# Plain fp32 products for the small matmuls of a hybrid decoder layer, regrouped between the projections

## The chip, the cores and the metric

The kernel runs on one NeuronCore of one Trainium2 chip. The metric is the device time of one execution, in microseconds (us). The times shown of the kernel before are 987.24, 990.89 and 992.40 us, with a median of 990.89 us. In the text, PE is the matrix engine (TensorE), DVE the vector engine, ACT the scalar engine, POOL the GpSimd engine, and SP the engine whose queue issues most of the transfers.

## The reference, cut to what matters

One decoder layer over 512 tokens plus 16 learned tokens (T = 528), of width 1024. One projection `h @ w_in` feeds two branches. The first is sliding-window attention with 16 query heads over 2 key heads. The second is RWKV-7 time mixing with 16 heads of 64 channels. Sigmoid gates merge the branches, and an output projection, a layer norm and a squared-ReLU MLP follow.

```python
w = -softplus(-(w0 + tanh(wl) @ w2)) - 0.5        # low-rank product, rank 64
a = sigmoid(a0 + al @ a2)                         # low-rank product, rank 64
g = sigmoid(gl) @ g2                              # gate product, rank 128
def step(S, inp):                                 # one token, one head, S is 64 x 64
    sa = einsum('bhij,bhj->bhi', S, -kk_t)
    S = S * w_t + sa * (kk_t * a_t) + v_t * k_t
    return S, einsum('bhij,bhj->bhi', S, r_t)
logits = einsum('nqkgd,nskd->kgnqs', qb, kw) * HEAD_DIM ** -0.5   # attention scores
merged = sigmoid(gate_att) * att + sigmoid(gate_rwkv) * rw
h = layer_norm(ALPHA * h + merged @ w_out)
h = layer_norm(ALPHA * h + square(relu(h @ w_ff1)) @ w_ff2)
```

All inputs are float32.

## The kernel before, in words

**Large products.** Every large matmul is a sum of three products of the type fp32r. Each operand is split into a part `hi` (a cast by ACT) and a rest `lo` (a subtraction by DVE), and `three` adds hi*hi, hi*lo and lo*hi in PSUM. The input projection runs as a generator `dense` for each block of 128 output columns: 24 matmuls of 512 columns for queries and gates, or two spans of 24 matmuls of 264 columns where the 16 extra tokens are needed too (keys, reads, values). Their PSUM tile is `dps`, from a pool `dn` of two banks.

**The recurrence.** It is computed in 8 chunks of 64 tokens, for a pair of heads at a time, so there are 8 pairs j. For a pair, `rwkv_scores` makes the products of scaled keys and queries inside each chunk (tile `sc`), `rwkv_inverse` inverts 16 x 16 triangles by a long row of small DVE instructions (tiles `ftmp`, `Xf`), `rwkv_blocks` joins them to 64 x 64 blocks (`up`), `rwkv_turn_inverse` makes `wp`, and `rwkv_fold` makes `gq` and adds it to `AX`. Then `rwkv_chain` passes a 64 x 64 state through the chunks: a link is two matmuls `ch`, and `follow` scales their results into `Z`, one half on DVE and one on ACT, for the next link.

**Small products beside it.** The low-rank products (`rwkv_lora`) keep hi and lo of an operand on the two halves of the partitions, so that two fp32r matmuls give what three would. The attention scores (`sp`) are made in the same way from `qs` and `khi`, `klo`; for `qs`, four transfers for each pair move halves of `qhi` and `qlo`. The gate product (`gp`) is a `three`. The small matmuls of the recurrence (`sc`, `gq`, `ch`, `wp`, `up`, `meta`, `Y`) are plain fp32, and the trace holds two records, two passes, for each of them. Transposes (`tr`, `axt`, `pt`, `yt`) have one.

**The order.** On PE it is written out by hand. A stage s works on pair s (`scan`), on pair s-1 (`solve`, and the attention scores) and on pair s-2 (attention output). `weave` walks through the stage's projection matmuls and puts each small job in when a running time has reached the job's number. That running time adds a fixed estimate for every projection matmul, so the number is a place among the projections, not a time of the clock. The other engines take their instructions in an order that the framework's scheduler derives, helped by `ahead(...)`.

```python
(5.6, (), F(rwkv_bonus, j)), (12.4, (), F(rwkv_turn_scores, j)),                          # L1395, L1396
(8.4, (), F(rwkv_fold, j, 0)), (10.6, (), F(rwkv_fold, j, 1)),                            # L1413
+ [(11.6 + 0.95 * c, (), F(rwkv_chain, j, c)) for c in range(NCH - 1)]                    # L1415
(7.4, (), F(rwkv_lora, j, 0)), (8.6, (), F(rwkv_lora, j, 1)),                             # L1423
items += attend(s - 1, 9.2) + join(s - 1, 11.6, 25.4, 0)[:2]                              # L1471
```

PSUM has eight banks: two for `dps` (`dn`), two called `g` (pool `pg`: `sc`, `gq`, `bp`, `wp`, `axt`, `tr`, `vt`), two called `a` (pool `pat`: `sp`, `pt`, `av`, `gp`, the low-rank products and some others) and two for the chain.

Of the kernel before, what the change touches and what calls it, by code (L numbers as in the profile page):

```python
# [31 lines left out]
PAIRS = HEADS // 2  # L32
DFF = 4096
# [51 lines left out]
ABUF = {'qs': 1, 'ga': 1, 'gg': 1, 'pa': 1, 'z': 1, 'bv': 1}  # L85
# [45 lines left out]
def hybrid_layer_kernel(ctx: ExitStack, tc: tile.TileContext, I: dict, out: bass.AP):  # L131
# [298 lines left out]
    zw = lz.tile([P, T], F32R, name="zw", tag="zw")  # L430
    za = lz.tile([P, T], F32R, name="za", tag="za")
    sghi = lz.tile([P, SEQ], F32R, name="sghi", tag="sghi")
    sglo = lz.tile([P, SEQ], F32R, name="sglo", tag="sglo")
# [11 lines left out]
    def low_rank(zl):  # L445
        twl = ew.tile([HD, T], F32, name="twl", tag="u")
        act.activation(twl, zl[0:HD], AF.Tanh)
        tal = ew.tile([HD, T], F32, name="tal", tag="L")
        act.copy(tal, zl[HD:P])
        for dst, src in ((zw, twl), (za, tal)):  # L450
            act.copy(dst[0:HD], src)
            dve.tensor_tensor(dst[HD:P], src, dst[0:HD].bitcast(F32), op=ALU.subtract)

    def gate_rank(zg):
        sg = ew.tile([P, SEQ], F32, name="sg", tag="v")
        act.activation(sg, zg[:, NMETA:], AF.Tanh, scale=0.5)
        dve.tensor_scalar(sg, sg, 0.5, 0.5, op0=ALU.mult, op1=ALU.add)
        act.copy(sghi, sg)
        dve.tensor_tensor(sglo, sg, sghi.bitcast(F32), op=ALU.subtract)
# [16 lines left out]
    def rwkv_begin(j):  # L476

        S = SS[j]
        lw = ew.tile([P, 2, P], F32, name="lw", tag="lw")
        lhi = ew.tile([P, 2 * P], F32R, name="lhi", tag="lhi")  # L480
        llo = ew.tile([P, 2 * P], F32R, name="llo", tag="llo")
        lf = lw.rearrange("p a c -> p (a c)")
        nc.sync.dma_start(lf, I["lora"][j])
        act.copy(lhi, lf)
        dve.tensor_tensor(llo, lf, lhi.bitcast(F32), op=ALU.subtract)
        S["lora"] = lhi, llo
# [3 lines left out]
    def rwkv_lora(j, q):  # L490
        S = SS[j]
        lhi, llo = S["lora"]
        zz, dst, bias = ((zw, S["tw"], "w0h"), (za, S["ta"], "a0h"))[q]
        qc = slice(q * P, (q + 1) * P)
        for t0, n in ALLT:
            ps = pat.tile([P, 512], F32, name="dps", tag="a")
            ts_ = slice(t0, t0 + n)
            pe.matmul(ps[:, :n], lhi[:, qc], zz[:, ts_], start=True, stop=False)
            pe.matmul(ps[:, :n], llo[:, qc], zz[:, ts_], start=False, stop=True)
            act.activation(dst[:, ts_], ps[:, :n], AF.Tanh, bias=dcol(bias, j), scale=0.5)  # L500
        if q == 0:
            tw = dst
# [100 lines left out]
    def rwkv_bonus(j):  # L603
# [3 lines left out]
        bp = pg.tile([P, 512], F32, name="bp", tag="g")  # L607
# [46 lines left out]
    def rwkv_scores(j, i):  # L654
# [9 lines left out]
        scs = [pg.tile([P, 512], F32, name="sc", tag="g") for e in range(2)]  # L664
# [7 lines left out]
        q4 = [ps.rearrange("p (c t) -> p c t", c=4) for ps in scs]  # L672
        with ahead(PRI["scores"]):
            for e in range(2):
                R = ER[e]
                dve.tensor_tensor(
                    NT[R, cs, :], q4[e][R, :, 0:C], B64(dv[R, cs], C), op=ALU.mult
                )
            for e in range(2):
                R, K_ = ER[e], ER[1 - e]  # L680
                dve.tensor_tensor(
# [1067 lines left out]
```

## Time and profile before

| what | value |
|---|---|
| median of three runs | 990.89 us |
| the profiled execution's own time | 988.82 us |
| its span | 986.7 us |
| PE busy | 943.9 us, 96% of the span |
| DVE busy | 654.9 us, 66% |
| ACT busy | 455.0 us, 46% |
| granted PE clock | 0.99 |
| low-rank products of a pair, PE records | 8 matmuls of 264 columns |
| attention scores of a pair, PE records | 16 matmuls of 256 columns |
| gate product of a pair, PE records | 3 matmuls of 512 columns |

The span is the time from the first to the last recorded instruction; 2.1 us of the execution's own time lie around it. A row of the groups shows a source line, engine, operation, the tiles (out<-in) and the shape, then the busy time of the group, the mean nanoseconds of one instruction and the idle time of the engine just before the group with what ended it. A row of the timeline shows start, duration, engine, line, operation, tiles, shape and how many instructions are merged in it. Matmuls overlap in the pipeline, so a matmul's duration is longer than its distance to the next one.

### The profile page before, as it was taken

The page shows a single profiled execution, that of the slowest core. Times are in us where ns is not written, and L with a number is a line of the kernel's source. Part 1 is how long each engine was busy: PE and PEld are TensorE (multiplying, and loading weights), DVE is VectorE, ACT ScalarE, POOL GpSimd, SP SyncE. Part 2 cuts the span into 40 slices and gives each one's busy share as a digit, 9 for nine tenths or more (in the row PEclk, how much of TensorE's full clock was granted, in tenths as well). Part 3 has the DMA queues.
Part 4 walks back from the last instruction along what each step waited for, and adds up shares of the span by engine and source line. Part 5 has one row for each costly group of instructions (what it writes and reads, how often), then busy time and mean ns, then how long its engine had stood idle before and what let it go on. Part 6 is the DMA issues. An engine that isn't in the chain of part 4 may idle for free.

```text
span 986.7 us, 19121 instructions
## 1 busy us (share of the span) xinstructions
PE 943.9 (96%) x7557; PEld 790.8 (80%) x7557; DVE 654.9 (66%) x1505; ACT 455.0 (46%) x1130; POOL 45.9 (5%) x108
## 2 busy tenths in 40 slices
PE   4999999999999999999999999999999999999996
PEld 3889878788888887888876778888888888888885
DVE  8677887888887888778786967666523244452427
ACT  6635447465473664654726834644412133442220
POOL 2000000010010000100001001000000000000001
PEclk9999999999999999999999999999999999999998
DMA  7545323233324432242534536133232323223222
GB/s 272 95 131 150 90 73 105 82 77 98 91 74 120 105 98 59 69 111 80 147 116 105 194 114 228 44 122 113 89 103 86 106 86 104 89 88 104 76 96 85
DMA packets 82673, 105.46 MB, mean 107 GB/s; under 512 B 47766, under 2 KB 54664, under 8 KB 82584
## 3 DMA queue, kind: packets, MB, share of 16 engines
q1 hardware_dynamic: 81088, 102.16, 35.0%
q10 hardware_dynamic: 1496, 2.08, 0.6%
q8 instruction: 59, 0.97, 0.4%
q14 instruction: 30, 0.25, 0.1%
HBM read 86.29 MB, written 13.74 MB: 101 GB/s over the span
## 4 chain that ended last, share of the span: by engine, by line
PE 72%; DVE 16%; ACT 5%; DMA 3%; issue 2%; POOL 2%; SPq 0%; DVEq 0%; ACTq 0%; POOLq 0%
PE dps L340 12%; PE dps L341 11%; PE dps L342 11%; PE acc L1518 6%; PE acc L1520 6%; PE acc L1519 6%; DVE wlo L259 3%; DMA wraw<-in_w_in_dram 2%; PE sc L668 2%; PE o L1292 1%; PE av L1196 1%; PE wp L873 1%; POOL grs L973 1%; PE ch L950 1%; PE o L1293 1%
## 5 line engine op out<-in xcount | busy, mean ns | idle before, releaser
L259 DVE TENSOR_TENSOR wlo<-wraw,whi 128x512 fp32r<-128x512 f32 x240 | 158.4, 686 | 178.2 <-ACT whi L256 177.4
L256 ACT CAST whi<-wraw 128x512 fp32r<-128x512 f32 x240 | 140.5, 616 | 271.8 <-PE dps L341 131.2
L340 PE MATMUL dps<-hhi,whi 128*128 128x264 f32 (+1 forms) x640 | 217.7, 340 | 7.3 <-DVE qlo L1074 5.5
L341 PE MATMUL dps<-hlo,whi 128*128 128x264 f32 (+1 forms) x640 | 204.5, 320 | 1.1 <-DVE hlo L321 1.1
L342 PE MATMUL dps<-hhi,wlo 128*128 128x264 f32 (+1 forms) x640 | 204.1, 319 | 0.4 <-DVE wlo L259 0.4
L340 PEld LDWEIGHTS dps<-hhi,whi 128*128 128x128 f32 x640 | 121.5, 190 | 22.2 <-DVE qlo L1074 6.8
L342 PEld LDWEIGHTS dps<-hhi,wlo 128*128 128x128 f32 x640 | 121.4, 190 | 9.1 <-DVE wlo L259 0.6
L341 PEld LDWEIGHTS dps<-hlo,whi 128*128 128x128 f32 x640 | 121.8, 190 | 7.3 <-DVE hlo L321 1.9
L341 PE MATMUL dps<-h1lo,whi 128*128 128x512 f32 (+1 forms) x256 | 97.5, 381 | 0.0
L340 PE MATMUL dps<-h1hi,whi 128*128 128x512 f32 (+1 forms) x256 | 97.5, 381 | 0.0
L342 PE MATMUL dps<-h1hi,wlo 128*128 128x512 f32 (+1 forms) x256 | 97.5, 381 | 0.0
L341 PEld LDWEIGHTS dps<-h1lo,whi 128*128 128x128 f32 x256 | 48.1, 188 | 10.2
L342 PEld LDWEIGHTS dps<-h1hi,wlo 128*128 128x128 f32 x256 | 48.1, 188 | 10.2
L340 PEld LDWEIGHTS dps<-h1hi,whi 128*128 128x128 f32 x256 | 48.1, 188 | 10.2
L1518 PE MATMUL acc<-whi,hhi 128*128 128x512 f32 x128 | 50.6, 395 | 0.0
L1519 PE MATMUL acc<-wlo,hhi 128*128 128x512 f32 x128 | 50.4, 394 | 0.0
L1520 PE MATMUL acc<-whi,hlo 128*128 128x512 f32 x128 | 50.2, 392 | 0.0
L1520 PE MATMUL acc<-whi,flo 128*128 128x512 f32 x112 | 44.0, 393 | 0.0
L1518 PE MATMUL acc<-whi,fhi 128*128 128x512 f32 x112 | 43.8, 391 | 0.0
L1519 PE MATMUL acc<-wlo,fhi 128*128 128x512 f32 x112 | 43.8, 391 | 0.0
L908 ACT ACTIVATE Z<-ch,PC 64x64 f32<-64x64 f32 x56 | 17.4, 310 | 41.0 <-PE ch L950 40.5
L1618 DVE TENSOR_TENSOR rl<-rl 128x512 f32<-128x512 f32 (+1 forms) x36 | 22.8, 632 | 15.2 <-ACT hhi L1617 9.1
(302 smaller groups left out, 1732.6 us busy)
## 6 DMA issues: line engine op xcount, KB each, us to landing
wraw<-in_w_ff_dram SPq DMA_DIRECT2D x64, 512.0 KB, 3.5
wraw<-in_w_in_dram SPq DMA_DIRECT2D x52, 512.0 KB, 3.6
wraw<-in_w_out_dram SPq DMA_DIRECT2D x8, 512.0 KB
xt<-in_x_dram SPq DMA_DIRECT2D x4, 512.0 KB, 7.5
Nd<-NT SPq DMA_DIRECT2D x16, 128.0 KB, 3.0
bv<-bv SPq DMA_DIRECT2D x8, 256.0 KB, 2.1
bvm<-bv SPq DMA_DIRECT2D x8, 256.0 KB
qs<-qhi SPq DMA_DIRECT2D x16, 128.0 KB, 2.2
```

The costliest lines, as they stand in the source:

```text
L256: act.copy(hi[:n, qs], raw[:n, qs])
L259: dve.tensor_tensor(lo[:n, qs], raw[:n, qs], hi[:n, qs].bitcast(F32), op=ALU.subtract)
L340: pe.matmul(ps, whi, xhi, start=first, stop=False)
L341: pe.matmul(ps, whi, xlo, start=False, stop=False)
L342: pe.matmul(ps, wlo, xhi, start=False, stop=last)
L668: pe.matmul(scs[e][:, c * P : (c + 1) * P], BK[ER[e], 4 * i + c, :], AXg[ER[e], e, 4 * i + c], start=True, stop=True,)
L873: pe.matmul(w4[:, c, :], XB[:, 4 * i + c, :], S["AT"][:, 4 * i + c, :], start=True, stop=True,)
L908: act.activation(dst, src[e][ER[e]], AF.Copy, scale=scale)
L1518: pe.matmul(acc[b], xhi[k][:, bs], hi[:, ws], start=first, stop=False)
L1519: pe.matmul(acc[b], xhi[k][:, bs], lo[:, ws], start=False, stop=False)
L1520: pe.matmul(acc[b], xlo[k][:, bs], hi[:, ws], start=False, stop=last)
L1618: dve.tensor_tensor(r, r, r, op=ALU.mult)
```

## The change

It has six parts.

1. **Plain operands.** The low-rank products, the attention scores and the gate product use fp32 operands as they are. `zw`, `za`, `sghi`, `sglo`, `lhi`, `llo`, `gwh`, `gwl`, `khi`, `klo`, `qhi`, `qlo` and `qs` go, with the casts, subtractions and transfers that made them. The two low-rank products stand on the two halves of the partitions, and so do the two heads of a score.
2. **Quarters.** `rwkv_scores` makes its products in 64 x 64 quarters, so that the two head-diagonal quarters share one bank and the other two share the second. Four instructions on 64 partitions (`NT`, `GR`) become two on 128.
3. **Both folds in one place.** For the first seven pairs, the second half of `rwkv_fold` follows the first at once; its two banks come from the pool `pat`.
4. **Places.** The chain starts at 10.6 with a step of 1.05. Low-rank products, gate product, the transposes `axt` and the attention scores have numbers that put them behind a chain link. A score call does two blocks of 128 queries at once, so there are two calls for a pair, not four.
5. **The bonus product** `bp` moves to the place of `wp` and takes its bank from `pat`.
6. **Smaller things.** The value transposes `vp` move to 21.0, and `first_up` uses the new tiles' room.

```diff
-ABUF = {'qs': 1, 'ga': 1, 'gg': 1, 'pa': 1, 'z': 1, 'bv': 1}
+ABUF = {'q': 2, 'ga': 1, 'gg': 1, 'pa': 1, 'z': 1, 'bv': 1}
...
     def low_rank(zl):
-        twl = ew.tile([HD, T], F32, name="twl", tag="u")
-        act.activation(twl, zl[0:HD], AF.Tanh)
-        tal = ew.tile([HD, T], F32, name="tal", tag="L")
-        act.copy(tal, zl[HD:P])
-        for dst, src in ((zw, twl), (za, tal)):
-            act.copy(dst[0:HD], src)
-            dve.tensor_tensor(dst[HD:P], src, dst[0:HD].bitcast(F32), op=ALU.subtract)
+        act.activation(zz[0:HD], zl[0:HD], AF.Tanh)
+        act.copy(zz[HD:P], zl[HD:P])
...
     def rwkv_lora(j, q):
-        for t0, n in ALLT:
-            ps = pat.tile([P, 512], F32, name="dps", tag="a")
-            ts_ = slice(t0, t0 + n)
-            pe.matmul(ps[:, :n], lhi[:, qc], zz[:, ts_], start=True, stop=False)
-            pe.matmul(ps[:, :n], llo[:, qc], zz[:, ts_], start=False, stop=True)
+        t0, n = ALLT[q]
+        pss = [pat.tile([P, 512], F32, name="lps", tag="a") for e in range(2)]
+        for e in range(2):
+            pe.matmul(
+                pss[e][:, :n], S["lora"][ER[e]], zz[ER[e], ts_], start=True, stop=True
+            )
+        for ps, (dst, bias) in zip(pss, outs):
             act.activation(dst[:, ts_], ps[:, :n], AF.Tanh, bias=dcol(bias, j), scale=0.5)
-        if q == 0:
+        if q == 1:
...
-        bp = pg.tile([P, 512], F32, name="bp", tag="g")
+        bp = pat.tile([P, 512], F32, name="bp", tag="a")
...
         for c in range(4):
+            for d in range(2):
+                for e in range(2):
+                    to = ER[e ^ d]
+                    pe.matmul(
+                        scs[d][to, c * P : (c + 1) * P], BK[ER[e], 4 * i + c, to],
+                        AXg[ER[e], e, 4 * i + c], start=True, stop=True,
+                    )
-            for e in range(2):
-                pe.matmul(
-                    scs[e][:, c * P : (c + 1) * P], BK[ER[e], 4 * i + c, :],
-                    AXg[ER[e], e, 4 * i + c], start=True, stop=True,
-                )
...
-            gqs = [pg.tile([P, 512], F32, name="gq", tag="g") for e in range(2)]
+            pool_, tag = ((pg, "g"), (pat, "a"))[i and j < PAIRS - 1]
+            gqs = [pool_.tile([P, 512], F32, name="gq", tag=tag) for e in range(2)]
...
         def evict(ps, t0, n):
             with ahead(PRI["dense"]):
-                act.activation(hi, ps, AF.Copy, scale=HD**-0.5)
-                dve.scalar_tensor_tensor(
-                    lo, ps, HD**-0.5, hi.bitcast(F32), op0=ALU.mult, op1=ALU.subtract
-                )
+                act.activation(q, ps, AF.Copy, scale=HD**-0.5)
...
     def gate_out(j):
-        three(gp, *A["gw", j], sghi, sglo)
+        pe.matmul(gp, A["gw", j], sg, start=True, stop=True)
...
-            pe.matmul(s3[:, e], qs[e][:, blk], khi[:, win], start=True, stop=False)
-            pe.matmul(s3[:, e], qs[e][:, blk], klo[:, win], start=False, stop=True)
+        for d in range(2):
+            n = 2 * i + d
+            for e in range(2):
+                pe.matmul(
+                    sps[e][:, d * 256 : (d + 1) * 256], q[ER[e], n * P : (n + 1) * P],
+                    kk[ER[e], n * P : n * P + 256], start=True, stop=True,
+                )
...
-            (5.6, (), F(rwkv_bonus, j)),
-            (12.4, (), F(rwkv_turn_scores, j)),
+            (6.4, (), F(rwkv_bonus, j)),
+            (12.55, (), F(rwkv_turn_scores, j)),
...
-            (10.6, (), F(rwkv_fold, j, 1)),
-        ] + [(11.6 + 0.95 * c, (), F(rwkv_chain, j, c)) for c in range(NCH - 1)] + [
+            (8.4 + 2.2 * last, (), F(rwkv_fold, j, 1)),
+        ] + [(10.6 + 1.0 * last + 1.05 * c, (), F(rwkv_chain, j, c)) for c in range(NCH - 1)] + [
...
-            (7.4, (), F(rwkv_lora, j, 0)),
-            (8.6, (), F(rwkv_lora, j, 1)),
+            (11.65, (), F(rwkv_lora, j, 0)),
+            (12.7, (), F(rwkv_lora, j, 1)),
...
-                items += [(8.6, (), turn_heads)]
+                items += [(21.0, (), F(turn_heads, s // 4))]
             if 0 < s < PAIRS - 1:
-                items += attend(s - 1, 9.2) + join(s - 1, 11.6, 25.4, 0)[:2]
+                items += attend(s - 1, 14.8) + join(s - 1, 13.75, 25.4, 0)[:2]
```

Three places show how the order moves. The first is PE in a middle stage before the change, from the first half of the fold on; L498 and L499 are the low-rank product of `a`, L340 to L342 are projection matmuls.

```order
L890 MATMUL gq<-GR,WT 128x128 x8
L498 MATMUL dps<-za,lhi 128x264
L499 MATMUL dps<-za,llo 128x264
L498 MATMUL dps<-za,lhi 128x264
L499 MATMUL dps<-za,llo 128x264
L340 MATMUL dps<-hhi,whi 128x512
L341 MATMUL dps<-hlo,whi 128x512
L342 MATMUL dps<-hhi,wlo 128x512
L1138 MATMUL sp<-khi,qs_3938 128x256
```

After the change, the same stage has `gq` with 16 products in one row and no low-rank product near it. The low-rank product `lps` comes behind a later chain link, with the transposes `axt` ahead of the link:

```order
L695 MATMUL axt<-con,AX 128x128 x8
L939 MATMUL ch<-Z,AX 64x64
L939 MATMUL ch_4318<-Z,AX 64x64
L484 MATMUL lps<-zz,lw 128x264 x2
L341 MATMUL dps<-hhi,whi 128x264
L342 MATMUL dps<-hlo,whi 128x264
L343 MATMUL dps<-hhi,wlo 128x264
```

So four small fp32r matmuls among the projections have become two plain products behind a link.

The second place is PE around the gate product `gp`, which follows a chain link in both kernels. Before:

```order
L950 MATMUL ch<-Z,AX 64x64
L950 MATMUL ch_4460<-Z,AX 64x64
L340 MATMUL gp<-sghi,gwh 128x512
L341 MATMUL gp<-sglo,gwh 128x512
L342 MATMUL gp<-sghi,gwl 128x512
```

After the change it is one plain product behind the fourth link:

```order
L939 MATMUL ch<-Z,AX 64x64
L939 MATMUL ch_4318<-Z,AX 64x64
L1088 MATMUL gp<-sg,gw 128x512
L341 MATMUL dps<-hhi,whi 128x264
L342 MATMUL dps<-hlo,whi 128x264
L343 MATMUL dps<-hhi,wlo 128x264
```

The score matmuls `sp`, which stood among the projections behind the first fold, now follow the fifth and the seventh link in the same way.

The third place is DVE in that stage, at the last half of the fold (`AX<-AX,gq`) and the state scaling `Z` of the first chain link. Before:

```order
L775 TENSOR_TENSOR ftmp<-Xf,Nf 66x55
L259 TENSOR_TENSOR wlo<-wraw,whi 128x512
L779 TENSOR_TENSOR Xf<-Xf,ftmp 66x11x5
L1141 TENSOR_TENSOR sb<-sp,bias 128x256
L775 TENSOR_TENSOR ftmp<-Xf,Nf 66x48
L895 TENSOR_TENSOR AX<-AX,gq 128x8x64 x2
L906 TENSOR_SCALAR Z<-ch,PC 64x64
```

Now four additions stand close together, and five steps of the small inverse lie between the last of them and the first `Z`:

```order
L884 TENSOR_TENSOR AX<-AX,gq 128x8x64 x2
L762 TENSOR_TENSOR ftmp<-Xf,Nf 66x64
L766 TENSOR_TENSOR Xf<-Xf,ftmp 66x8x8
L884 TENSOR_TENSOR AX<-AX,gq 128x8x64 x2
L762 TENSOR_TENSOR ftmp<-Xf,Nf 66x63
L766 TENSOR_TENSOR Xf<-Xf,ftmp 66x9x7
L762 TENSOR_TENSOR ftmp<-Xf,Nf 66x60
L766 TENSOR_TENSOR Xf<-Xf,ftmp 66x10x6
L762 TENSOR_TENSOR ftmp<-Xf,Nf 66x55
L895 TENSOR_SCALAR Z<-ch,PC 64x64
```

On PE, six projection matmuls of 264 columns stand between the first and the second chain link after the change, where before the change there were nine and `gp`, `sp` and `axt`.

More of the change, by code (lines that the diff above doesn't have):

```diff
@@ L32 @@
 PAIRS = HEADS // 2
+ATT_GROUP = PAIRS // 2
 DFF = 4096
@@ L478, in rwkv_begin @@
         S = SS[j]
[L479 to L486, printed above, removed]
+        S["lora"] = lw = ew.tile([P, P], F32, name="lw", tag="lw")
+        nc.sync.dma_start(lw, I["lora"][j])
         S["tw"] = ew.tile([P, T], F32, name="tw", tag="tw")
@@ L1117, in evict @@
             A["gg", j] = t
-        A["gw", j] = gwh, gwl
+        A["gw", j] = gw
         yield from dense(COL_GRW + j * P, XT_, evict)
@@ L1402, in solve @@
     def solve(j):
+        last = j == PAIRS - 1
         return [
```

137 lines of the change are left out of this document (51 added, 86 removed).

## The prediction

> **What bounds the kernel now.** I read the page first, then the stages, then PE's groups with their idle time, and last the timeline of one middle stage. The page's first part, its chain, and one of the stretches of 120 us:
>
> ```profile
> PE 943.9 (96%) x7557; PEld 790.8 (80%) x7557; DVE 654.9 (66%) x1505; ACT 455.0 (46%) x1130; POOL 45.9 (5%) x108
> PE 72%; DVE 16%; ACT 5%; DMA 3%; issue 2%; POOL 2%; SPq 0%; DVEq 0%; ACTq 0%; POOLq 0%
> 240.00:360.00 120.00, 116.82 (x1233) 99.71 (x1217) 98.42 (x266) 70.64 (x202) 8.94 (x22) 1.00 0.33 89
> ```
>
> PE works 116.8 of 120 us there at a granted clock of 1.00, and DVE 98.4. So the time of this part is the distance from one PE start to the next, plus the few waits of PE. The change touches nothing behind the output projection. PE's groups show where it waited (the last columns):
>
> ```profile
> L340 PE MATMUL dps<-hhi,whi 128*128 128x264 f32 x448 | 135.8, 303 | 7.3 <-DVE qlo L1074 5.5 <-ACT whi L256 1.1 <-DVE ftmp L775 0.6
> L1138 PE MATMUL sp<-khi,qs 128*128 128x256 f32 x64 | 17.3, 296 | 5.1 <-ACT ta L500 2.7 <-DVE sb L1141 1.8 <-DMA qs<-qlo 0.7
> L1054 PE MATMUL vp<-con,vT 64*128 64x64 f32 x10 | 1.0, 227 | 2.9 <-issue 1.5 <-ACT ta L500 1.5
> L498 PE MATMUL dps<-zw,lhi 128*128 128x264 f32 x16 | 4.4, 292 | 1.4 <-DVE zw L452 1.4
> ```
>
> Two of these return stage by stage; the first twice, a stage apart, with what ended it, and a case of the second:
>
> ```profile
> 230.47 0.60 ACT L1073 ACTIVATE qhi<-dps 128x512 fp32r<-128x512 f32 x1
> 231.12 0.68 DVE L1074 SCALAR_TENSOR_TENSOR qlo<-dps,qhi 128x512 fp32r<-128x512 f32 x1
> 231.86 0.39 PE L340 MATMUL dps<-hhi,whi 128*128 128x264 f32 x1 [0.91 <-DVE qlo L1074]
> 295.60 0.39 PE L340 MATMUL dps<-hhi,whi 128*128 128x264 f32 x1 [0.91 <-DVE qlo L1074]
> 323.19 0.84 ACT L500 ACTIVATE ta<-dps,drv 128x264 f32<-128x264 f32 x2
> 323.71 0.39 PE L1138 MATMUL sp<-khi,qs 128*128 128x256 f32 x1 [0.67 <-ACT ta L500]
> ```
>
> The projection after a query waits until DVE has emptied the query's bank, and the scores wait for a bank of `pat` that the low-rank product still holds.
>
> **Prices.** Plain products, fp32r products and the gaps around an island of small ones:
>
> ```profile
> 314.82 1.95 PE L873 MATMUL wp<-AT,XB 128*128 128x128 f32 x16
> L873 PE MATMUL wp<-AT,XB 128*128 128x128 f32 x128 | 15.6, 275 | 0.0
> 318.52 0.29 PE L498 MATMUL dps<-zw,lhi 128*128 128x264 f32 x1
> 319.02 0.39 PE L340 MATMUL dps<-hhi,whi 128*128 128x512 f32 x1
> 320.18 0.39 PE L342 MATMUL dps<-hhi,wlo 128*128 128x512 f32 x1
> 320.50 1.16 PE L890 MATMUL gq<-GR,WT 64*128 64x128 f32 x16
> 321.59 0.39 PE L498 MATMUL dps<-za,lhi 128*128 128x264 f32 x1
> 321.81 0.29 PE L499 MATMUL dps<-za,llo 128*128 128x264 f32 x1
> 321.94 0.28 PE L498 MATMUL dps<-za,lhi 128*128 128x264 f32 x1
> 328.07 0.29 PE L342 MATMUL dps<-hhi,wlo 128*128 128x264 f32 x1
> 328.28 0.34 PE L950 MATMUL ch<-Z,AX 128*64 128x64 f32 x4
> 328.55 0.50 PE L340 MATMUL gp<-sghi,gwh 128*128 128x512 f32 x1
> 328.88 0.39 PE L341 MATMUL gp<-sglo,gwh 128*128 128x512 f32 x1
> 329.12 0.39 PE L342 MATMUL gp<-sghi,gwl 128*128 128x512 f32 x1
> 329.35 0.28 PE L340 MATMUL dps<-hhi,whi 128*128 128x264 f32 x1
> ```
>
> - fp32r: (329.35 - 328.88)/2 = 0.234 us for 512 columns; 321.94 - 321.81, 0.12 to 0.13, for 264; four of 264 take 319.02 - 318.52 = 0.50.
> - Plain: eight products are 16 passes. 1.95 less one duration of 0.275 is 1.675 us for 15 steps, 0.112 a pass of 128 columns. A product has two passes, so it costs 1.75 ns a column.
> - `gq` has 16 passes too, of 64 rows, and 1.16 - 0.28 = 0.88: two halves of the array run together.
> - Entry and exit: from 320.18 to 321.81 are 1.63; less one step of 512 and one of 264 the island is 1.28. Its eight double passes are 0.90, so 0.38 goes for the two switches. For the link, 328.07 to 328.88 less 0.12 and 0.234 is 0.46; its own passes (two double ones of 64 columns) are 0.11, the switches 0.35.
>
> **The change part by part.**
> *Folds together:* one island less for seven pairs, 7 x -0.38 = -2.7.
>
> *Low-rank products:* 16 islands, as before 16 groups of 0.50. Now two double passes of 264 columns, 264 x 1.75 ns = 0.46. They use another shape of the array than the link before them, so I add one more switch, half of 0.38. Twelve stand behind a link: 0.46 + 0.19 - 0.50 = +0.15 each. Four stand without one (two in the stretch before the first stage, two in the first stage) and pay both switches: +0.34 each. Sum +3.2. Bounds: the switch is free (-0.04 each), or all 16 pay both (+0.34).
>
> *Scores:* for two blocks, eight matmuls of 0.12 = 0.96 become four double passes of 256 columns, 0.90, and a switch of 0.19: +0.13, 16 times, +2.1 (bounds -0.06 and +0.32 each).
>
> *Gate product:* 512 columns, 0.90 against three of 0.234 = 0.70, 8 times: +1.6.
>
> *Quarters:* 16 products of 64 x 64 for eight of 64 x 128, so twice the passes with the same 128 columns. If four quarters run together the time is the same, 0.90; if only two do, it doubles. The nearest rows are those of `up`, which uses four small tiles:
>
> ```profile
> L822 PE MATMUL up<-X,NT 16*32 16x16 f32 x512 | 5.8, 180 | 0.0
> ```
>
> Here 5.8 us for 512 passes is 11 ns each, where one pass of 16 columns at 0.875 ns would take 14 alone. So tiles do overlap, but the row cannot tell two at a time from four. I take zero, since rows (`gq`) and columns of the array (the link's two halves) are each seen to run in parallel; the other end, +0.90 for each of 16 calls, is a rival. `bp` between `wp` and `av` I take as zero, because `gp` above follows a link with no more than the switch that is counted (bound +0.38, 8 times); `axt` before a link too.
>
> Work of PE: -2.7 + 3.2 + 2.1 + 1.6 = **+4.2 us**.
>
> *Waits removed:* with `qlo` gone, the bank is free when ACT's copy ends. ACT's `qhi` ended at 231.07, 0.7 before `qlo`, so a wait of 0.1 to 0.3 could stay; but the copy now stands behind six exponentials of the scores, which come later. The matmuls of the next span cover it (24 x 0.12 = 2.9 us). If that cover fails, the old 0.91 is back, six times. I take all 5.5 as gained. The scores now come well behind the low-rank products (2.7), the copies of `qs` are gone (0.7), `vp` moves to a place where no low-rank product holds the banks (2.9), and at the start two operations in a row fall away behind `zw` (1.3 of 1.4). SP issues 37 transfers fewer by its order; apart from the 0.7, no wait in the rows above hangs on its queue. Sum **-13.1 us**; bounds -13 and -7. The savings on DVE (`qlo`, `llo`, `gwl`, two `NT` and `GR` a call) and on ACT count only through these waits.
>
> *Where a stall goes:* DVE's work between `av` and the first `Z`, in the order shown above. Its rows:
>
> ```profile
> 317.84 0.69 DVE L1202 SCALAR_TENSOR_TENSOR ga<-ga,av 128x512 f32<-128x512 f32 x1
> 318.56 0.69 DVE L1217 TENSOR_TENSOR z<-z,ga 128x512 f32<-128x512 f32 x1
> 319.17 0.19 DVE L775 TENSOR_TENSOR ftmp<-Xf,Nf 66x39 f32<-66x39 f32 x1
> 320.10 0.21 DVE L775 TENSOR_TENSOR ftmp<-Xf,Nf 66x55 f32<-66x55 f32 x1
> 322.83 1.27 DVE L895 TENSOR_TENSOR AX<-AX,gq 128x512 f32<-128x512 f32 x2
> 317.72 0.50 PE L340 MATMUL dps<-hhi,whi 128*128 128x512 f32 x1
> ```
>
> A step of the inverse takes (320.10 - 319.17)/4 = 0.23 when it waits only for itself. I put the new order on this clock. `bp` now lies ahead of `av`, so `ga` starts at 317.84 + 0.47 = 318.3, and the inverse continues at 319.6. Eleven steps (2.6), two additions (1.27), two steps (0.5), two additions (1.27) and five steps (1.2) follow: the first `Z` starts at 326.4 and ends 0.25 later. PE: projections resume at 317.72 + 0.47 = 318.2; nine of 512 with 0.2 of entry put `gq` at 320.5; its 16 double passes end at 322.5; nine more put the first link at 324.8 and, after its 0.27 and six matmuls of 264 with their gaps (0.9), the second at 325.95. It waits for `Z` until 326.65, **0.7 us**. In the five middle stages that have `ga` and `z` this is +3.5; bounds 0 (the inverse runs ahead) and 1.4 each. Behind the waiting link stand the low-rank product and all projections; ACT's `tw`, and then the scan on DVE, come that much later, with 33 projection matmuls before the keys need them. The second bank of the scores waits for DVE's `gg`, about +0.1, six times: +0.6. The folds' banks of `pat` are free by then: `bv` and `ga` end at 319.0, `gq` reaches them at 321.4.
>
> **Sum:** 4.2 - 13.1 + 3.5 + 0.6 = -4.8. The span goes from 986.7 to 981.9 and this execution's own time from 988.82 to 984.0. That execution was 2.1 below the median of the runs shown; on the median, 990.89 - 4.8 = **986.1 us**.
>
> **Rivals.**
> 1. *The quarters run two at a time.* 16 x 0.90 = +14.4, so 990.89 - 4.8 + 14.4 = 1000.5, slower. For it: no row shows four tiles of this size together. Against it: two at a time is seen both along rows and along columns. It decides from 0.6 us more a call on. [...] Chance 0.10.
> 2. *The stall only moves.* The second link waits 1.4 instead of 0.7 (+3.5) and the query's copy comes late behind the exponentials (+5.5): 990.89 - 4.8 + 9.0 = 995.1. For it: DVE has 98 of 120 us. Against it: three operations less a stage there, and 2.9 us of cover. Chance 0.15.
> 3. *No stall and cheap switches.* The inverse runs ahead (-3.5), and the second switch costs nothing (28 x 0.19 = -5.3): 977.3. Chance 0.16.
> 4. *Plain products at half the price,* one pass time for both: `gp` -0.45 x 8, low-rank -0.23 x 16, scores -0.45 x 16, together -14.5, so 971.6. The rows of `wp` speak against it, since its second passes are recorded apart. [...] Chance 0.03.
>
> **How the numbers follow.** The forecast has 0.56, with its own range from 982 to 990. What a measurement can tell from no change is about 0.5%, 5 us, so faster means below 985.9. Of the forecast's 0.56 a half (0.28) lies below that, with rivals 3 and 4 this is 0.47. Slower is rival 1 and a third of rival 2, 0.15. The rest, 0.38, is no change. The range runs from 977 to 996: it takes in rivals 2 and 3 and leaves out 1 and 4 and some of the edges.
>
> **What would show it.** Right: no row of `qlo`; PE's idle time before `dps` and `sp` near zero; `gq` as one row of 32 passes over some 2.0 us; the second link of a middle stage with an idle time of some 0.7 ended by DVE `Z`; `sc` with 32 passes in the time that 16 took. Wrong: `sc` near 2 us a call; a stage (63.74 us from 231.86 to 295.60 above) longer than that with no wait in it, which would mean that switches or plain passes cost more than I took; or a new wait in front of `dps` behind the exponentials.

## The result, and the profile after

The changed kernel took 975.69 us (median of 4 runs, 974.94 to 976.25) against 989.07 of the kernel before beside it: a ratio of 0.9882 with a 95% interval from 0.9856 to 0.9908. The forecast was 986.1, faster by 4.8; it became faster by 13.4 by these medians and by 11.7 by the ratio. The sign held and the size did not. On the 990.89 of the forecast the ratio gives 979.2, inside the range from 977 to 996 but near its end; the median itself, 975.69, lies 1.3 below it. In the experiments below one execution of the kernel before, beside the z runs, took 2286 us, and the ratios leave it out. The profiled execution has a span of 973.4 us and a time of 975.15 (before: 986.7 and 988.82). First the page of the changed kernel (busy time of each engine; shares of the chain that ended last), then its groups of PE's work (count, busy time, mean of one, idle time ahead and what ended it):

```profile
PE 941.4 (97%) x7805; PEld 776.7 (80%) x7805; DVE 633.6 (65%) x1444; ACT 449.2 (46%) x1111; POOL 45.8 (5%) x106
...
PE 84%; DVE 10%; DMA 2%; ACT 2%; issue 1%; POOL 0%; SPq 0%; DVEq 0%; ACTq 0%; POOLq 0%
```

```profile
L341 PE MATMUL dps<-hhi,whi 128*128 128x264 f32 x448 | 136.0, 304 | 1.1 <-ACT whi L257 1.0 <-DVE k L416 0.2
L1102 PE MATMUL sp<-kk,q 64*128 64x256 f32 x128 | 19.4, 403 | 0.0
L939 PE MATMUL ch<-Z,AX 128*64 128x64 f32 x224 | 18.8, 246 | 2.9 <-DVE Z L895 2.9
L659 PE MATMUL sc<-AX,BK 64*64 64x128 f32 x512 | 18.1, 275 | 1.0 <-DVE AX L672 1.0
L879 PE MATMUL gq<-GR,WT 64*128 64x128 f32 x256 | 16.7, 279 | 0.0
L1088 PE MATMUL gp<-sg,gw 128*128 128x512 f32 x16 | 9.0, 643 | 1.2 <-issue 1.2
L833 PE MATMUL up<-X,NT 32*32 32x32 f32 x256 | 6.6, 192 | 2.3 <-DVE X L828 2.3
```

Three of these groups in the kernel before:

```profile
L668 PE MATMUL sc<-AX,BK 64*128 64x128 f32 x256 | 19.0, 285 | 0.9 <-DVE AX L685 0.9
L950 PE MATMUL ch<-Z,AX 128*64 128x64 f32 x224 | 18.8, 246 | 0.6 <-DVE Z L906 0.6
L846 PE MATMUL up<-X,NT 32*32 32x32 f32 x256 | 5.8, 192 | 0.4 <-DVE X L841 0.4
```

Of the 7.3 us ahead of `dps` 1.1 are left, and the 5.1 ahead of `sp` are gone; `ch` and `up`, which hardly waited, now have 2.9 and 2.3. `sc` has twice the instructions and no more time. A middle stage, in the timeline of PE (start, duration, instruction, idle time ahead):

```profile
313.14 2.06 PE L879 MATMUL gq<-GR,WT 64*128 64x128 f32 x32
315.12 0.50 PE L341 MATMUL dps<-hhi,whi 128*128 128x512 f32 x1
...
318.40 0.28 PE L343 MATMUL dps<-hhi,wlo 128*128 128x264 f32 x1
319.09 0.34 PE L939 MATMUL ch<-Z,AX 128*64 128x64 f32 x4 [0.41 <-DVE Z L895]
319.35 0.71 PE L484 MATMUL lps<-zz,lw 64*128 64x264 f32 x4
...
324.14 0.28 PE L343 MATMUL dps<-hhi,wlo 128*128 128x264 f32 x1
324.35 0.34 PE L939 MATMUL ch<-Z,AX 128*64 128x64 f32 x4
324.61 1.13 PE L1088 MATMUL gp<-sg,gw 128*128 128x512 f32 x2
325.17 0.68 PE L341 MATMUL dps<-hhi,whi 128*128 128x264 f32 x1
325.70 0.29 PE L342 MATMUL dps<-hlo,whi 128*128 128x264 f32 x1
...
326.77 0.34 PE L939 MATMUL ch<-Z,AX 128*64 128x64 f32 x4
327.03 1.24 PE L1102 MATMUL sp<-kk,q 64*128 64x256 f32 x8
```

Both folds stand in one row of 2.06 us, the second link waits 0.41 for DVE's `Z`, and gate product and scores ride on a link. An island's cost is read from the last projection ahead to the second one behind, less two steps: 325.70 - 324.14 - 0.24 = 1.32 for a link with the gate product.

Then there is a row that the prediction never asked for. The windows of the profiled execution of the kernel before, one microsecond each (stretch; its length, PE's busy time; granted clock; DMA share, GB/s):

```profile
128.00:129.00 1.00, 0.14 (x2) 1.00 0.03 8
129.00:130.00 1.00, 0.39 (x5) 1.00 0.00 0
130.00:131.00 1.00, 1.00 (x7) 1.00 0.00 0
131.00:132.00 1.00, 1.00 (x7) 0.59 0.22 66
132.00:133.00 1.00, 1.00 (x5) 0.50 0.20 66
133.00:134.00 1.00, 1.00 (x4) 0.50 0.00 0
```

Behind the wait of `vp` the granted clock was 0.50 for 3.41 us; a second such stretch began at 73 us. In these two a projection step takes 0.22 us for 264 columns and 0.43 for 512, in place of 0.12 and 0.23. If PE does half the work in it, each costs half its length, 1.7 us. So I split every span in three: PE's idle time (the sum of its idle times above 0.15 us), half of the time at half clock, and the rest, which I call PE's work. Every profile also ends with a stretch at half clock, 2.1 us behind the end of PE's last product in the kernel before and in the changed one; it is not counted as lost. The 7.4 to 8.2 us behind that product are part of the work.

| profiled execution | span | PE idle | lost at half clock | work |
|---|---|---|---|---|
| before, as the prediction read it | 986.7 | 34.96 | 3.41 | 948.3 |
| changed | 973.4 | 24.35 | 0 | 949.0 |
| difference | -13.3 | -10.6 | -3.4 | +0.7 |

The forecast had -9.0 for the waits, +4.2 for the work, nothing for the clock.

### The profile page after: what moved, and what is told of

It is laid out like the page before. It is cut to its first block, busy times and chain, and to the rows that moved or that the text cites. A ratio compares the mean times of both kernels' runs of the same rounds, so it can differ in the third digit from the quotient of the medians.

```text
span 973.4 us, 19464 instructions
## 1 busy us (share of the span) xinstructions
PE 941.4 (97%) x7805; PEld 776.7 (80%) x7805; DVE 633.6 (65%) x1444; ACT 449.2 (46%) x1111; POOL 45.8 (5%) x106
## 4 chain that ended last, share of the span: by engine, by line
PE 84%; DVE 10%; DMA 2%; ACT 2%; issue 1%; POOL 0%; SPq 0%; DVEq 0%; ACTq 0%; POOLq 0%
PE dps L341 15%; PE dps L342 14%; PE dps L343 14%; PE acc L1488 6%; PE acc L1489 6%; PE acc L1490 6%; PE sp L1102 2%; PE av L1165 2%; PE o L1261 2%; PE sc L659 2%; DVE AX L884 1%; PE ch L939 1%; DVE ftmp L762 1%; DVE wlo L260 1%; PE o L1262 1%; PE o L1263 1%
## 5 line engine op out<-in xcount | busy, mean ns | idle before, releaser
L342 PE MATMUL dps<-hlo,whi 128*128 128x264 f32 (+1 forms) x640 | 203.5, 318 | 0.8 <-DVE hlo L322 0.7
L342 PEld LDWEIGHTS dps<-hlo,whi 128*128 128x128 f32 x640 | 120.7, 189 | 8.9 <-DVE hlo L322 1.6
L342 PE MATMUL dps<-h1lo,whi 128*128 128x512 f32 (+1 forms) x256 | 97.3, 380 | 0.0
L342 PEld LDWEIGHTS dps<-h1lo,whi 128*128 128x128 f32 x256 | 48.0, 187 | 10.3
L1588 DVE TENSOR_TENSOR rl<-rl 128x512 f32<-128x512 f32 (+1 forms) x36 | 22.8, 632 | 14.9 <-ACT hhi L1587 9.0
L762 DVE TENSOR_TENSOR ftmp<-Xf,Nf 66x15 f32<-66x15 f32 (+7 forms) x120 | 24.7, 206 | 7.2 <-DMA Nf<-Nd 4.7
```

The source lines that it names most:

```text
L342: pe.matmul(ps, whi, xlo, start=False, stop=False)
L762: dve.tensor_tensor(tv, Xf[:, 0:nj, s : s + 1].to_broadcast([NB, nj, nt]), Nf[:, s : s + 1, s + 1 :].to_broadcast([NB, nj, nt]), op=ALU.mult,)
L1588: dve.tensor_tensor(r, r, r, op=ALU.mult)
```

## The experiments

Each kernel ran beside the kernel before on the same chip, whose medians were 987.54, 986.27 and 987.24 in the three groups (x, y, z). Ratios are to those, with 95% intervals; the changed kernel itself has 0.9882.

### Is the clock a property of the program? (x1)

No edit: the kernel before, again.

> The kernel before the change, unaltered, run again with a profile. The profiled execution of it that the prediction read had two stretches of 3.41 us each at half clock (74 and 131 us after the span's start), each right behind a stretch in which PE stood still for 0.9 to 1.5 us; the profile of the changed kernel has none. They make 3.4 of the 13.3 us between the two spans. Theory C (the clock): the stretches come or stay away by where the stall falls on a grid of 3.41 us that runs freely, so the granted clock of these runs varies (0.993 to 0.997), and the time with it, about 1.7 us for each 0.0017. Theory P (the program): the stretches belong to the two stalls, so all runs have 0.994 and the profile shows both at the same places. Theory W (waits and work alone, as in the prediction): the clock explains nothing, and what the forecast lacked is in the islands of small products and in the waits.

988.12 us (12 runs, 985.66 to 992.06), ratio 1.0005 (0.9989 to 1.002). The granted clock ranged from 0.992 to 0.998 and the span with it, from 989.9 down to 983.5. The profiled execution was one at 0.998, without a stretch at half clock ahead of the last: idle 35.2, work 948.3. The theory of the clock holds, that of the program falls: with the same program the time lost to the clock varies by up to 6 us from one execution to the next. Without the clock the change is 983.5 - 973.4 = 10.1 us. This profile also shows what a stop costs beside its idle time:

```profile
227.58 0.28 PE L342 MATMUL dps<-hhi,wlo 128*128 128x264 f32 x1
228.78 0.39 PE L340 MATMUL dps<-hhi,whi 128*128 128x264 f32 x1 [0.92 <-DVE qlo L1074]
229.01 0.28 PE L341 MATMUL dps<-hlo,whi 128*128 128x264 f32 x1
229.13 0.28 PE L342 MATMUL dps<-hhi,wlo 128*128 128x264 f32 x1
```

From 227.58 to 228.78 are 1.20: 0.92 idle, 0.12 for the step, and 0.16 more; the next step takes 0.23 in place of 0.12. So a stop in a run of fp32r products costs 0.27 beyond the idle time that the row shows. The six stops behind a query all show nearly these two numbers.

### What was the query's bank worth? (x2, x3)

```diff
                 act.activation(q, ps, AF.Copy, scale=HD**-0.5)
+                lo = at.tile([P, SEQ], F32, name="qlo", tag="spl")
+                dve.scalar_tensor_tensor(
+                    lo, ps, HD**-0.5, q, op0=ALU.mult, op1=ALU.subtract
+                )
```

> The changed kernel, with one operation of DVE put back behind ACT's copy of a query: it reads the query's bank once more (0.69 us), as the one before did, into a tile that nobody reads. Theory of the prediction: the bank is held 0.7 us longer, so the projection after a query waits 0.91 again, six times: 975.7 + 5.5 = 981.2. Rival (it only moves): PE's new waits for DVE and ACT behind it (the second chain link, 0.41 five times) take up the delay, less than +2. Rival (DVE is near its limit): the six operations more make DVE late elsewhere too, over +8.

975.98, ratio 0.9881 (0.986 to 0.9902): nothing lost. The groups of this run:

```profile
L341 PE MATMUL dps<-hhi,whi 128*128 128x264 f32 x448 | 137.1, 306 | 3.2 <-DVE qlo L1056 2.2 <-ACT whi L257 1.0
L833 PE MATMUL up<-X,NT 32*32 32x32 f32 x256 | 5.5, 192 | 0.0
```

The wait came back, but at 2.2 us in place of 5.5, and the 2.3 ahead of `up` went: while PE stood at the bank, DVE caught up. PE's instructions are the same as in the changed kernel, so the two timelines can be laid side by side: each of the six stops takes about 0.26 us beyond its idle time, and in each of four stages the removed waits of `up` had taken 0.27 to 0.30 beyond theirs. The rival "it only moves" is right, though the place is `up` and not the second link, whose 2.9 stayed. Why 2.2 and not 5.5 is in the timelines, first of the kernel before (x1), then of this run: the query's last product, ACT's copy, DVE's operation, the projection that waits.

```profile
224.55 0.39 PE L342 MATMUL dps<-hhi,wlo 128*128 128x512 f32 x1
...
227.40 0.60 ACT L1073 ACTIVATE qhi<-dps 128x512 fp32r<-128x512 f32 x1
```

```profile
223.26 0.39 PE L343 MATMUL dps<-hhi,wlo 128*128 128x512 f32 x1
...
225.34 0.60 ACT L1054 ACTIVATE q<-dps 128x512 f32<-128x512 f32 x1
226.25 0.68 DVE L1056 SCALAR_TENSOR_TENSOR qlo<-dps,q 128x512 f32<-128x512 f32 x1
226.98 0.39 PE L341 MATMUL dps<-hhi,whi 128*128 128x264 f32 x1 [0.42 <-DVE qlo L1056]
```

ACT's copy stands behind exponentials now, as the prediction said, but starts 2.1 us after the query's last product started, where it was 2.85 before (there it stood behind two others, one of which waited for DVE).

The second edit does the operation twice.

> The same with the operation done twice, so the bank is held 1.4 us longer. Theory of the prediction: each wait grows to about 1.6 us, six times: 975.7 + 9.6 = 985.3, granted clock 0.997. Theory C: a stall of 1.6 us is as long as the one of 1.47 us behind which the kernel before had a stretch at half clock, so some of the six are followed by 3.41 us at half clock: 1.7 us more for each, 987 to 995, granted clock 0.987 to 0.995.

985.17, ratio 0.9974 (0.996 to 0.9988): +9.5. The six waits are 9.6 together, as the sum has them:

```profile
L341 PE MATMUL dps<-hhi,whi 128*128 128x264 f32 x448 | 136.5, 305 | 10.6 <-DVE qlo L1059 9.6 <-ACT whi L257 1.0
```

The total agrees with the sum partly by chance: the idle time rose by 8.8 (to 33.1), since the 2.3 of `up` went again and `gp` waits 1.1 longer, 1.7 went at half clock, and the work is 0.9 less. The theory of the clock, in the form that any stall of 1.6 us opens it, fell: none of these six did. One stretch at half clock stands behind a wait of 2.3 us of `gp`. So a term of waits has a threshold: the first 0.7 us more on the bank cost nothing, the second 0.7 cost 9 us.

### The second link's wait (x4), and up's (y4)

```diff
-            (12.55, (), F(rwkv_turn_scores, j)),
+            (12.90, (), F(rwkv_turn_scores, j)),
-        ] + [(10.6 + 1.0 * last + 1.05 * c, (), F(rwkv_chain, j, c)) for c in range(NCH - 1)] + [
+        ] + [(10.6 + 1.0 * last + 1.05 * c + 0.35 * (c > 0 and not last), ...
-            (11.65, (), F(rwkv_lora, j, 0)),
-            (12.7, (), F(rwkv_lora, j, 1)),
+            (12.0, (), F(rwkv_lora, j, 0)),
+            (13.05, (), F(rwkv_lora, j, 1)),
-                items += attend(s - 1, 14.8) + join(s - 1, 13.75, 25.4, 0)[:2]
+                items += attend(s - 1, 15.15) + join(s - 1, 14.10, 25.4, 0)[:2]
```

> The changed kernel, with the second and the later chain links, the low-rank products, the gate product, the scores and the turn of AX each due 0.35 later, so that one span of three projection matmuls (0.37 us) more stands between the first link and the second. Theory of the prediction: the second link's wait for DVE's Z (0.41 in five stages, 0.91 in the first) goes, and nothing takes its place: -2.0 to -2.4, 973.4. Rival (it only moves): DVE's chain is what the links follow, and the wait turns up at a later link or at Y: 975.7. Rival (late scores and low-rank products): ACT's tw and the scan come later and PE waits at the keys: +1 or more.

973.08, ratio 0.9852 (0.9832 to 0.9872): -2.6, as the waits say. The five waits of 0.41 are gone, the first stage's stayed. The profiled execution is the slowest of the five (974.67): its idle time is 23.0, 1.3 less than in the changed kernel, and 1.7 us went at half clock at 27 us, so it does not show the whole 2.6.

```profile
L939 PE MATMUL ch<-Z,AX 128*64 128x64 f32 x224 | 18.8, 246 | 1.1 <-DVE Z L895 0.9
```

For y4 all five items due at 3.2 (`rwkv_meta`, the second `rwkv_scores`, `rwkv_inverse`, `rwkv_blocks` and `rwkv_start` of step 2) are due at 3.6 as well.

> The kernel with the chain links one span later (973.1), and beside it all that was due at 3.2 (the third step of the inverse, up, with the scan's second half) due at 3.6, one span of 0.70 us later. Theory of the prediction (time is work plus waits): the waits of up for DVE's X (0.42 and 0.16 in four stages) go: -2.4, 970.7. Rival (it only moves): the next up or av waits for U or for the scores instead: 973.

971.94, ratio 0.9848 (0.9823 to 0.9874), the fastest of all; the forecast was 970.7.

```profile
L939 PE MATMUL ch<-Z,AX 128*64 128x64 f32 x224 | 18.8, 246 | 2.0 <-DVE Z L895 2.0
L833 PE MATMUL up<-X,NT 32*32 32x32 f32 x256 | 6.2, 193 | 0.0
```

The 2.3 of `up` went, 0.9 returned at the links (0.26 in five stages) and 1.0 ahead of `dps` (one wait of 1.54 for DVE's `k`, 0.48 in x4): so a large part of the gain only moved. x4 and y4 were measured beside different chips; by their ratios alone they can't be told apart.

### What the quarters are worth (y1, z1, z4)

y1 takes the quarters back, products and the operations that empty the banks:

```diff
-            for d in range(2):
-                for e in range(2):
-                    to = ER[e ^ d]
-                    pe.matmul(
-                        scs[d][to, c * P : (c + 1) * P], BK[ER[e], 4 * i + c, to],
-                        AXg[ER[e], e, 4 * i + c], start=True, stop=True,
-                    )
+            for e in range(2):
+                pe.matmul(
+                    scs[e][:, c * P : (c + 1) * P], BK[ER[e], 4 * i + c, :],
+                    AXg[ER[e], e, 4 * i + c], start=True, stop=True,
+                )
...
```

> The changed kernel with the products of the scan (sc) as before the change: eight of 64 rows by 128 columns a call in place of sixteen quarters, and six operations of DVE to empty the two banks in place of four. Theory of the prediction, as the traces corrected it: PE's work is the same (an island with sc took 2.66 before and 2.61 after), and DVE's two operations more a call (0.42 each) count only where PE waits for DVE behind them: the waits of up (0.43 and 0.16, four stages) grow by 0.8 each: 975.7 + 3.4 = 979.1. Rival (PE gains from the quarters): no island differs by more than 0.1 by the traces, so it would have to be a wait; 975.7 if DVE has room. Rival (the quarters run two at a time, refuted by the rows): would make this faster than 975.7 by up to 14.

987.75 (10 runs, 985.52 to 992.88), ratio 1.0017 (0.9997 to 1.0037): +12.1, where the waits gave +3.4. With this one part undone the whole change is worth nothing. The wait of `up` grew as expected, by 0.8 in four stages, and two more stages wait 0.5; first such a wait in the changed kernel, then in this run, then this run's group and its windows:

```profile
298.77 0.22 PE L833 MATMUL up<-X,NT 32*32 32x32 f32 x2 [0.43 <-DVE X L828]
```

```profile
238.74 0.21 PE L834 MATMUL up<-X,NT 32*32 32x32 f32 x2 [1.26 <-DVE X L829]
```

```profile
L834 PE MATMUL up<-X,NT 32*32 32x32 f32 x256 | 7.0, 192 | 7.1 <-DVE X L829 7.1
```

```profile
237.00:238.00 1.00, 0.48 (x3) 1.00 0.61 234
238.00:239.00 1.00, 0.21 (x2) 1.00 0.02 8
239.00:240.00 1.00, 0.89 (x38) 1.00 0.00 0
240.00:241.00 1.00, 1.00 (x15) 0.93 0.00 0
241.00:242.00 1.00, 1.00 (x12) 0.50 0.02 1
242.00:243.00 1.00, 1.00 (x8) 0.50 0.02 1
```

Two microseconds behind the wait the clock is at 0.50. This execution took 989.8 us and lost 8.5 of them to four such stretches, three of 3.41 us and one of 6.83, and each begins 1.2 to 2.3 us behind an `up` that had waited 1.25; its idle time is 30.1 (+5.8) and its work 949.4 (+0.4). Five of the ten runs show a granted clock of 0.995 and take 985.5 to 986.7, so they lost less to the clock.

z1 is y1 with the items of 3.2 at 3.6: the same wide products, 0.70 us more projection ahead of `up`.

> The kernel with the wide products of the scan (987.8 us, five stretches of 3.41 us at half clock in its profile, each 2 us behind an up that had waited 1.25 us for DVE's X), and beside it all that was due at 3.2 due at 3.6, one span of 0.70 us of projections later. Theory C (the wait of up next to an island of small products lets the clock fall, and that is most of what the wide products cost): the waits shrink from 1.25 to about 0.5, the window has more projection in it, the stretches go: 977 to 980, granted clock 0.996 or more. Rival (the wide products or their two operations cost by themselves): above 985.

979.71, ratio 0.9928 (0.991 to 0.9947), granted clock 0.998 to 0.999. The waits of `up` fell to 0.55, those of the links grew from 0.41 to 0.63, no stretch at half clock is left ahead of the last, and 8.0 us came back:

```profile
L834 PE MATMUL up<-X,NT 32*32 32x32 f32 x256 | 6.8, 192 | 2.8 <-DVE X L829 2.8
```

The idle time is 27.2, 2.9 less than in y1, so about 5 of the 8.0 us are the clock. Of the 12.1 us of y1 about half went to waits of PE for DVE and about half to the clock behind them; the wide products themselves added 0.4 to 0.8 us of work. In the profiled execution of y1 the clock has the larger part, 8.5 us.

z4 puts the quarters alone into the kernel before.

> The kernel before the change, with the quarters alone (products of the scan and the four operations that empty their banks). In the changed kernel the quarters are worth 12 us, by the waits of up. Theory (waits): before the change PE stands still at the query's bank ahead of up, DVE is in time there (no wait of up in the middle stages), so two DVE operations less a call bring nothing: 986 to 988. Rival (the quarters gain by themselves): 980 or less. Rival (PE pays for twice the passes): above 990.

986.43, ratio 0.9994 (0.9981 to 1.0006): no difference, as the theory of waits says. Its idle time is 35.0, as before. There `up` hardly waits, and x2 shows that a stop at the query's bank is enough for that; what DVE saves has no one who waits for it.

### Folds apart (y2)

```diff
-        last = j == PAIRS - 1
+        last = True
...
-            pool_, tag = ((pg, "g"), (pat, "a"))[i and j < PAIRS - 1]
+            pool_, tag = pg, "g"
```

> The changed kernel with the two folds of a pair apart (the second 2.2 later and in the same two banks as the first) and the chain links one step later, as before the change; the rest as changed. Theory of the prediction, with the prices of the traces: seven islands more at 0.41 each, +2.9, and the second link's waits for DVE's Z (0.41 five times and 0.91) go, -3.0: 975.7. Rival (the island is all that counts, the wait moves): +2.9, 978.6. Rival (apart is better, since DVE adds the first fold while PE multiplies the second): -2 or more, below 974.

974.79, ratio 0.9878 (0.9847 to 0.9909), so no difference, as the two terms said.

```profile
L939 PE MATMUL ch<-Z,AX 128*64 128x64 f32 x224 | 18.8, 246 | 0.7 <-DVE Z L895 0.7
L879 PE MATMUL gq<-GR,WT 64*128 64x128 f32 x256 | 18.7, 284 | 0.0
```

The work rose by 3.3 (952.3; seven islands at 0.41 are 2.9), the idle time fell by 3.2 (21.1). Putting the folds together saved work and paid for it with the links' waits; only with the links one span later (x4) is something left.

### The gate product (y3), all three together (z2)

```diff
-        pe.matmul(gp, A["gw", j], sg, start=True, stop=True)
+        three(gp, *A["gw", j], sghi, sglo)
```

(with the conversions of both operands as before the change)

> The changed kernel with the gate product as three fp32r products in place of one plain one (and ACT's and DVE's conversions of its operands back, two operations of about 0.2 us a stage). By the traces a link with the gate product is an island of 1.16 us with three fp32r products and of 1.32 with the plain one. Theory of the prediction (the plain product costs more on PE): -0.16 x 8 = -1.3, 974.4. Rival (the conversions make ACT or DVE late): 975.7 to 977. Rival (plain products are cheaper than priced, a reason for the gain that was missed): slower than 975.7 by more than 1.

974.69, ratio 0.9877 (0.9852 to 0.9902), expected 974.4. Its span is 0.8 below the changed kernel's (work -0.7, idle -0.1). It agrees with the price of the islands, but -1.0 between two groups of runs is not secured.

> The kernel with links and up later (971.9), and beside it the gate product as three fp32r products (-1.0 where it was tried alone). If work and waits add up: 970.9. Rival (ACT and DVE have less room now that the links no longer wait): 972 or more.

972.42, ratio 0.9855 (0.9835 to 0.9875): not faster than y4's 0.9848. Whether the gate product gains anything beside the other two stays open; its profiled execution has less work (947.2) and one stretch at half clock.

### The turn of the values alone (z3)

```diff
-                items += [(8.6, (), turn_heads)]
+                items += [(21.0, (), F(turn_heads, s // 4))]
```

(in the kernel before, with the values kept by key head)

> The kernel before the change, with one move alone: the turn of the values (vp) at 21.0 in place of 8.6, where no low-rank product holds the banks. Theory of the prediction: its two waits (1.47 each) go, -2.9, and nothing else: 984.5. Theory C: behind the first of them the kernel before has a stretch at half clock in some of its executions; so the spread of its times (985 to 992) shrinks too and its median falls by more than 2.9. Rival (it only moves): the low-rank products or the scores take up the wait, 987.

985.53, ratio 0.9982 (0.9972 to 0.9993): -1.7 in place of -2.9. Both waits of 1.47 are gone, but in the same two stages the scores now wait 0.78 and 0.72. The row names nothing that ended the wait; that it is the bank is inferred from the other stages, where a wait of 0.67 at this place ends with ACT's `ta`:

```profile
131.34 0.36 PE L1138 MATMUL sp<-khi,qs 128*128 128x256 f32 x1 [0.78 <-issue]
```

The idle time is 32.6, 2.4 less than before, so the waits explain the gain and a little more. The stretch at 131 us is gone, but this profile has one at 75 us and another at 27, and eight of its ten runs have a granted clock of 0.993 or 0.994, where two of the 18 beside it have so little. So the expected gain from the clock did not come: the runs spread from 982.91 to 986.27, those of the kernel before beside it from 985.04 to 988.57.

## Why the prediction was right, and where its size failed

The sign was right for the reason given: waits of PE went, and they were worth more than what came in their place. That the range held by the ratio is partly luck, since rival 3 set its lower end and neither reason of that rival came true.

- **What bounds the kernel: right, with a term missing.** Spans are work plus waits plus the clock: over 11 of the 12 profiles of the experiments the work is 947.2 to 949.8, whatever the waits; y2, with its seven islands, has 952.3. The missing term is the granted clock. The 1.00 of "at a granted clock of 1.00" was read in 120 us of the middle; the window from 50 to 150 us had 0.97, and the prediction did not use it. That is 3.4 of the 8.9 us by which this pair of executions differs more than forecast (13.7 in their own times against 4.8); 3.5 are in the work, 1.6 in the waits and 0.4 around the span.
- **Waits removed, -13.1: measured -14.9.** `qlo` 5.5, `vp` 2.9, `zw` 1.4, and all 5.1 of `sp`, of which I had left 1.8 (`sb`, the last pair). But "I take all 5.5 as gained" had the wrong cause: DVE's operation was worth nothing by itself (x2), ACT's earlier copy halved the wait, and what PE gained at the bank it paid in part at `up`.
- **New waits, +4.1: measured +5.7** (`ch` +2.4, `up` +1.9, `gp` +1.2, `pt` +0.2, the waits of before subtracted). The second link was the right place at 0.41 in place of 0.7; the first stage, at 0.91, was not in the sum. The scores' second bank never waited (+0.6 was wrong). `up` and `gp` were not seen: asked what is late next, I followed DVE from `av` to `Z` and stopped, where the next one was the transpose for `up` 43 us on. The rest of the difference, about -1.4, is in small waits at the start and behind the projections.
- **Work, +4.2: measured +0.7, against either profile of before.** This is the step that was mis-sized most. The islands of the two kernels, term by term:
  - folds 2.18 for 2 x 1.29, -0.41 (forecast -0.38);
  - a low-rank product behind a link +0.21, behind `axt` and a link +0.13, alone +0.35 (forecast +0.15, +0.15, +0.34);
  - the scores of two blocks 1.16 for 0.95, +0.21 (+0.13), and the gate product 0.86 for 0.69, +0.16 (+0.2);
  - `bp` between `wp` and `av` 3.47 for 3.00 + 0.47, and `sc` within 0.06: zero, as said.

  Together that is about +5. The sum lacked two things. The first is the price of a stop: 0.27 for each of 13 stops in fp32r products (six behind a query, six ahead of scores, one behind `zw`), -3.5. New stops give a part of it back: about 0.28 in each of four stages at `up` (x2), +1.1, and only 0.07 at a link (319.09 - 318.40 - 0.12 - 0.41 = 0.16 against 324.35 - 324.14 - 0.12 = 0.09), where the entry to the island costs 0.09 without any stop. The second lies where the prediction says "The change touches nothing behind the output projection". From the output projection's first product to PE's last one there are 2144 products in both kernels. Without the idle time they take 421.3 us in all four profiles built on the kernel before and 419.5 to 420.0 in all ten built on the changed one: -1.4 us, which no run explains. About one microsecond stays open beside that. PE's first products run at half rate, too, up to 19.8 to 22.8 us after the start (in the kernel before the steps of the transposes `tp` are 0.21 us there, and 0.11 from 614 us on), which by an estimate from these times moves the work by up to 1.4 us from profile to profile.
- **Rivals.** Quarters two at a time: refuted, 512 instructions take 18.1 us where 256 took 19.0; a call's 32 passes take 1.10 us, where two at a time would need 16 x 0.112 = 1.79. The four quarters of a chunk, two to a bank, start within 0.03 us of each other (63.98 to 64.01 us in the first call). Plain products at half the price: refuted, the gate product is 0.86, forecast 0.90. "The stall only moves" was right in kind (x2, y2, y4, z3) and wrong in size. "No stall and cheap switches" came nearest in time (977.3), but neither of its reasons held: the link waits, and a second shape costs about 0.2 (+0.21 for a low-rank product behind a link, where -0.04 stood for a free switch).

## What to carry to other kernels

Make the sum over one engine of three terms, its work, its waits and what its clock does behind the waits, and split two profiles in the same way before explaining their difference. Price a stop at more than the idle time that is shown, and ask of each removed wait which other engine used it to catch up. The same two DVE operations a call are worth nothing in one kernel, where nobody waits for them (z4), and with what the clock adds 12 us in the next (y1), so try the parts of a change one at a time from both ends.

## What the hardware showed that was not expected

**The clock can fall behind a stop of 1.25 us, where small products stand beside it.** In these profiles all stretches at half clock between the start and the end last 3.41 us, or 6.83 once (y1), and begin on a grid of 3.41 us (in the kernel before at 73.15 and 131.18 us, 17 lengths of 3.413 apart). Waits of 1.25 us were enough (y1), and six of 1.6 us did nothing (x3). What tells them apart I worked out from all 14 profiles: in each of the 3893 windows of the grid between start and end I added, for the matmuls that start in it, columns x time per column (about 0.44 ns for fp32r, from steps of 0.227 us for 512 columns of `acc` in the changed kernel; 0.875 for a plain pass, from 0.112 us for 128 columns of `wp`) x active rows / 128, as a share of the window.

| share of the window | windows | followed by half clock |
|---|---|---|
| up to 0.375 | 10 | 10 |
| 0.39 to 0.43 | 13 | 3 |
| 0.44 and more | 3870 | 0 |

A product of 32 rows counts a quarter in this measure, so an island of `up` and its neighbours has little to set against a wait beside it, while a stop among projections of 128 rows leaves enough. Without the rows the measure does not separate them (windows up to 0.71 fell, others at 0.41 did not). The measure is mine and was fitted after the fact; no run varied the rows alone, so that the rows are the cause is not shown.

**A stop has its own price:** 0.27 us beyond the idle time in a run of fp32r products (x1), and 0.26 for the six stops of x2 beside the changed kernel.
